# A hybrid decoder layer on one core: x's tiles loaded in another sequence, and the table of priority shifts replaced for all three stages

## Chip, core and metric

The kernel runs on one core of a Trainium2 chip. A core has TensorE (matrix products, PE in the profile), VectorE (DVE), ScalarE (ACT), GpSimd (POOL), SyncE (SP, which issues most transfers), and 16 DMA engines between the chip's main memory and the core's memories, SBUF for operands and PSUM for the results of TensorE. The metric is the time of one execution on the device in microseconds, here the median of three runs.

## The reference, cut to what matters

All data is float32. x is 1024 x 1024, and 16 meta tokens stand ahead of it, so 1040 rows go through one layer:

```python
h = rms_norm(x, pre_norm_g)
z = h @ W_in                                        # 1024 x 7328
pv, pg, cq, ckv, kr, mg, cu, cg, sbcx, sg, gl = split_cols(z)
y_a = (pool_mixer(pv) * silu(pg)) @ w_out_pool      # windows 2, 4, 8, 16, mean minus self
y_b = (mla_attention(cq, ckv, kr) * silu(mg)) @ w_out_mla    # 8 heads, causal softmax
y_c = (conformer_conv(cu) * silu(cg)) @ w_out_conf  # width 31, LayerNorm, swish
y_d = (short_conv(sbcx) * silu(sg)) @ w_out_sc      # width 3
g = sigmoid(gl + gate_bias)                         # four gates for each channel
out = x + rms_norm((g0*y_a + g1*y_b + g2*y_c + g3*y_d) @ W_o, post_norm_g)
```

## The kernel before

**Products.** A float32 operand is split into a high part (rounded to the format that TensorE multiplies fast, `fp32r` in the profile) and a low part, the rest. `split` lets ACT copy the high part and another engine, POOL where nothing is said, subtract for the low part. A product then takes three matmuls: high by high, high by low, low by high. The two large products, with W_in and W_o, use a scheme of Strassen's kind: seven products of blocks instead of eight, whose operands are blocks or sums of blocks.

**Stage 1** (up to the first `plan.flush()`, L1579) loads x in eight tiles of 128 rows (`load_x`, L903) and the meta tokens. `parts` (L957) handles one or more tiles: `square` (L934) forms the sum of squares on ACT (`junk` in the profile), POOL forms the reciprocal root, `scaled` lets DVE scale the tile (`x<-x,rsx,ps`), and `operand_of` (L946) transposes it on TensorE (`ps_x` and `ps_y` from `ident,x`), with the high part copied by ACT and the low part subtracted by DVE. Tiles 0 to 3 go into the operands B11 and B21, tiles 4 to 7 into B12 (whose memory is also called T3) and B22. `sums_of` (L969) forms the sums for T1, T2 and T4 on POOL and DVE. Then come

- `plain` (L779): the columns of `ckv` and `kr`, with eight products in the banks `ps_pa` and `ps_pb` for each of two column ranges, U0 and U1 (256 columns, and 256 with the 16 of the meta tokens). Within a range it goes through (B11, B21), tiles 0 to 3, and then (B12, B22), tiles 4 to 7.
- 28 pairs of weight blocks. `prep` (L693) splits the weights of a pair (`A` and `S` in the profile, sums `ss` and `raw` on DVE, low parts on POOL), and `unit` (L734) runs the seven products into `ps_pa`, `ps_pb`, `ps_pc` and `ps_pd`; DVE and ACT take the results (`u`, `z`). The last pair's results, gates, go to memory tiles `zlast`, which POOL stores.
- side work between the units: the convolutions, the query and key columns, the pool tasks (`task_pool`, L1232: POOL adds shifted rows `sa` and `sb`, DVE subtracts, `ps_y<-sa,pv` and `ps_y<-sb,pv`), and others.

**Stage 2** (up to L1878) is attention over 8 heads and two halves of the queries (`attend`, L1684): scores into five banks `ps_s`, ACT's exponential `p`, its split `pt`, products with `vt` into the one bank `ps_o`, which ACT copies out (`ol`). Key blocks of 128 end in one of 16 rows (`100x16`). Between them TensorE does the output products of the three other branches (`ps_y<-bo,whl`). Stage 2's memory overlies stage 1's: `ol` lies where `zlast` was. **Stage 3** is the product with W_o, the second norm and the output.

**What sets the order.** No line issues an instruction at once. `Plan.record` (L352) notes each operation with its number, an estimated cost and what it depends on; the whole program is recorded so, and issued through one line, L389, which is why all rows of the profile name it. `flush` (L549) orders the operations of a stage by a simulation of the five engines: whenever an engine is free, it takes, among the operations that are ready by the modelled times, the one with the lowest priority number. That is the operation's number, less a lift that `plan.ahead(n)` gives. The table SHIFTS then adds to the numbers of single operations or runs of them: an entry is (first operation in the stage, how many, engine or None for all, by how much). Before, it has 55 entries for stage 2 and 7 for stage 3, none for stage 1. Where TensorE has nothing ready and the first pair's units are not over yet, the simulation puts filler transposes into its order, up to eight in a row (`keep_busy`, L307; `ps_w<-ident`).

On the chip every engine runs its list in the order that came out of this, and waits where an operand, a bank or a slot of memory isn't there yet.

Of the kernel before, what the change touches and what calls it, by code (L numbers as in the profile page):

```python
# [23 lines left out]
BF16 = mybir.dt.bfloat16  # L24
AF = mybir.ActivationFunctionType
ALU = mybir.AluOpType
# [4 lines left out]
P = 128  # L31
D = 1024
# [21 lines left out]
C_CU, C_CG, C_SC, C_SG, C_GL = 1440, 1952, 2208, 2976, 3232  # L54
# [8 lines left out]
B11, B21, B22, T1, T2, T3, T4 = range(7)  # L63

B12 = T3
# [6 lines left out]
def f(ap):  # L72
    return ap.bitcast(F32)

SHIFTS = {
    2: [
        (515, 16, "PE", -400), (164, 16, "PE", 60), (1048, 32, None, -5), (1358, 64, "DVE", 5),  # L80
        (1663, 8, None, 150), (1490, 64, "POOL", -5), (1072, 32, "DVE", -5), (1524, 16, "POOL", -150),
        (1874, 2, None, 60), (144, 2, "PE", 20), (886, 16, "DVE", 5), (660, 16, "PE", 20), (1595, 32, "PE", -60),
        (1866, 2, "PE", 150), (1322, 16, "DVE", -5), (1186, 8, "PE", -60), (1425, 8, None, -150),
        (1014, 32, "DVE", -400), (1874, 4, "ACT", -60), (15, 4, "SP", -20), (1916, 4, None, -60),
        (1936, 4, None, -20), (1299, 64, "PE", -5), (1492, 16, None, 20), (1323, 4, "DVE", 20), (1492, 1, None, 5),
        (1642, 32, "PE", -5), (1090, 2, "DVE", 20), (1907, 32, "POOL", 400), (901, 1, "DVE", 400),
        (1762, 16, "PE", -400), (1849, 32, None, -60), (1784, 16, "PE", 60), (182, 8, "PE", -400),
        (1903, 8, "PE", 150), (1582, 4, "PE", 20), (1237, 1, None, -20), (252, 2, "DVE", 400),
        (1491, 16, "PE", -150), (890, 64, "POOL", -20), (133, 8, "PE", -150), (980, 4, None, 5),
        (1938, 2, None, 150), (1291, 4, "PE", -150), (1496, 64, "PE", 5), (968, 16, None, -20),  # L90
        (1206, 32, "POOL", -400), (653, 64, "PE", -5), (1617, 32, "PE", 20), (1764, 32, "DVE", 60),
        (1691, 8, "PE", -400), (1596, 64, "PE", -20), (1847, 16, "PE", 20), (1332, 2, None, -400),
        (1218, 16, "PE", 20),
    ],
    3: [
        (433, 16, "PE", -20), (139, 16, "POOL", 400), (860, 32, "DVE", -150), (814, 32, "PE", 60),
        (600, 8, "PE", 60), (809, 16, "DVE", 400), (762, 2, None, -20),
    ],
}

# [139 lines left out]
class Plan:  # L240
# [308 lines left out]
    def flush(self):  # L549
# [9 lines left out]
        self.phase += 1  # L559
        for a, n, eng, by in SHIFTS.get(self.phase, ()):  # L560
            for o in ops[a:a + n]:
# [10 lines left out]
def trunk_kernel(ctx, tc, a):  # L572
    nc = tc.nc
    plan = Plan(nc)
    PE, ACT, DVE, POOL, SP = (plan.engine(e) for e in ("PE", "ACT", "DVE", "POOL", "SP"))
# [10 lines left out]
    def copy(out, in_, scale=1.0):  # L586
        ACT.activation(out, in_, AF.Copy, scale=scale)

    def sub(eng, out, x, y):
        eng.tensor_tensor(out, x, y, op=ALU.subtract)  # L590
# [7 lines left out]
    def split(hi, lo, src, eng=None):  # L598
        copy(hi, src)
        sub(eng or POOL, lo, src, f(hi))  # L600
# [65 lines left out]
    tp = pool(one, name="tp", reuse_waits="tile")  # L666
# [18 lines left out]

        return wp.tile([P, KH, 2 * P], F32, tag="raw", bufs=3, name=name)

    def blk(src, name):
        b = wp.tile([P, 2, KH, P], F32R, tag="blk", bufs=7, name=name)
        split(b[:, 0], b[:, 1], src)  # L690
        return b

    def prep(c):  # L693

        (a11, a21), (a12, a22) = ((t[:, :, :P], t[:, :, P:]) for t in (wload(0, c), wload(1, c)))
        ss = raw("ss")
        s1, s2 = ss[:, :, :P], ss[:, :, P:]  # L700
        add(DVE, s1, a21, a22)
        sub(DVE, s2, s1, a11)
        sub(DVE, a21, a11, a21)
        w = {n: blk(src, n) for n, src in (("A11", a11), ("S2", s2), ("S1", s1), ("S3", a21))}
        sub(DVE, s2, a12, s2)
        w.update({n: blk(src, n) for n, src in (("A12", a12), ("A22", a22), ("S4", s2))})
        return w

    def product(ps, w, b, c0, n, start, stop):
# [66 lines left out]
            out(0, 1, pc, u2[:, :nb], u2)  # L776
        pump()

    def plain(w, c0, n, out):  # L779

        for j, bs in enumerate(((B11, B21), (B12, B22))):
            for i, m in enumerate((P, 64)):
                ps = bank(("pa", "pb")[i])[:m, :n if j == 0 else min(n, 512 - c0)]
                for h, b in enumerate(bs):
                    (product, stacked)[i](ps, w[h][i], b, c0, n, h == 0, h == 1)
                with plan.ahead(EVAC):
                    out(i, j, ps, None, None)
# [113 lines left out]
    xt = {}  # L901

    def load_x(t):  # L903

        xt[t] = (t4([P, D], name="x") if t in (4, 5, 6, 7) else
                 wp.tile([P, D], F32, tag="raw", bufs=3, name="x") if t == 0 else
                 wp.tile([P, D], F32, tag="blk", bufs=7, name="x"))
        for c in (slice(0, 512), slice(512, D)) if t == 0 else (slice(0, D),):
            SP.dma_start(xt[t][:, c], a["x"][0, P * t:P * (t + 1), c])
    g8 = tp.tile([KD, P], F32, tag="wraw", bufs=2, name="g8")  # L910

    with plan.slow(-2000):
        load_x(0)
        ACT.dma_start(g8, a["pre_norm_g"][0].rearrange("(k p) -> k p", p=P))
        load_x(1)
        load_x(4)
        load_x(5)
        raw_kv = [wload(i, C_CKV, P + 32) for i in range(2)]
        for t in (2, 6, 3, 7):
            load_x(t)  # L920
        xm = wp.tile([NM, D], F32, tag="blk", bufs=7, name="xm")
        SP.dma_start(xm, a["meta_tokens"])
# [8 lines left out]
    ssx = const.tile([P, 16], F32, name="ssx")  # L931
    rsx = const.tile([P, 16], F32, name="rsx")

    def square(x_, t):  # L934
        n = x_.shape[0]
        ACT.activation(tp.tile([P, D], BF16, tag="whl", name="junk")[:n], x_, AF.Square, accum_out=ssx[:n, t:t + 1])

    def scaled(x_, t):
        n = x_.shape[0]
# [14 lines left out]
        copy(HB[b][:, 0, :, c], p3)  # L954
        sub(DVE, HB[b][:, 1, :, c], p3, f(HB[b][:, 0, :, c]))

    def parts(*ts):  # L957

        r0 = turn[1]
        turn[1] += len(ts)  # L960
        for i, t in enumerate(ts):
            square(xt[t], r0 + i)
        rsqrt_mean(rsx[:, r0:r0 + len(ts)], ssx[:, r0:r0 + len(ts)], D, eng=POOL)
        for i, t in enumerate(ts):
            scaled(xt[t], r0 + i)
            for j, b in enumerate(((B11, B21), (B12, B22))[t // 4]):
                operand_of(b, t % 4, xt[t][:, 512 * j:512 * (j + 1)])
# [36 lines left out]
    U0, U1 = (0, 256), (256, 256 + NM)  # L1004

    def nopump():
        pass
    parts(0)
    parts(1)

    w_kv = [[blk(t[:, :, :P], "kv")] for t in raw_kv]
    kr = wp.tile([P, 2, KH, 64], F32R, tag="blk", bufs=7, name="kr")
    for i, t in enumerate(raw_kv):
        split(kr[:, i, :, :32], kr[:, i, :, 32:], t[:, :, P:P + 32])
        w_kv[i].append(kr[:, i])
    parts(4, 5)
    out_kv = [out_raw(("ckv", "kr"), *u) for u in (U0, U1)]
    parts(2, 6)
    parts(3, 7)
    meta()  # L1020
    plain(w_kv, *U0, out_kv[0])
    for t in range(2):
        sums_of(t)
    w = prep((C_CU, C_CU + 256))
    for t in range(2):
        operand_of(T3, t, xt[t + 4][:, :512])
    for t in range(2, 4):
        sums_of(t)
    plain(w_kv, *U1, out_kv[1])
    for t in range(2, 4):  # L1030
        operand_of(T3, t, xt[t + 4][:, :512])
    prow = w1([P, P], name="prow")
# [530 lines left out]
    for i, (_, names, kind) in enumerate(pairs):  # L1563
# [11 lines left out]
        w = nxt  # L1575
# [381 lines left out]
    for d in (0, 4, 1, 5, 2, 6, 3, 7):  # L1957
        whl = [wtile(ep, "w_out_mla", d, i) for i in range(2)]
        th = ep.tile([P, NT], F32, tag="th", bufs=3, name="th")
        ld(th, th_dram[8 + d])  # L1960
        for c in range(2):
            t = th[:, 512 * c:512 * (c + 1)]
            py = bank("u")
            for k in range(4):
                b = boM[c][k]
                w = whl[k // 2][:, :, k % 2]
# [154 lines left out]
```

## Time and profile before

| what | us |
|---|---|
| median of three runs | 962.89 (961.86 to 963.99) |
| the profiled execution | 961.49 |
| its span in the trace | 959.6 |
| TensorE busy | 943.1 |
| VectorE, ScalarE, GpSimd busy | 700.4, 451.8, 675.7 |
| DMA | 205.95 MB, 215 GB/s on average |

A row of a timeline reads: start and length in us, engine, line, operation, result<-operands, shape, how many in a row, and in brackets how long the engine had been idle and what released it. A group's row ends in busy us and mean ns of one, then the idle time ahead of it. `L389` is the recording line throughout.

### The profile page before, as it was taken

What the parts mean: (1) busy time and instruction counts of PE and PEld (TensorE: products, weight loads), DVE (VectorE), ACT (ScalarE), POOL (GpSimd) and SP (SyncE); (2) the same over time, 40 slices, a digit from 0 to 9 for tenths busy, and PEclk for the clock granted to TensorE, in tenths of its full rate; (3) what the DMA queues carried; (4) which work ended last, traced back from release to release, by engine and by line L of the source; (5) the groups of instructions that cost most, each with busy time, mean ns of one, the idle gap of its engine ahead of it and who ended that gap; (6) DMA issues with size and microseconds to landing.
All of it is one profiled execution on the core that took longest, in us unless ns stands there. A gap on an engine that the chain in (4) does not pass through costs nothing.

```text
span 959.6 us, 15213 instructions
## 1 busy us (share of the span) xinstructions
PE 943.1 (98%) x4944; PEld 803.2 (84%) x4944; DVE 700.4 (73%) x1124; ACT 451.8 (47%) x925; POOL 675.7 (70%) x627
## 2 busy tenths in 40 slices
PE   8999999999999999999999999989999999999996
PEld 7998999988888888888888888868888888888885
DVE  5855988896998898555665558437868887898656
ACT  7753344334443454554554443256465564325622
POOL 5957677557877776778876886456368796847955
PEclk9999999999999999999999999999999999999998
DMA  8146556666688959868696578798978864783533
GB/s 262 42 127 204 148 185 216 219 216 230 227 254 266 315 189 279 243 186 240 213 281 186 148 238 294 221 293 241 292 210 270 209 209 127 259 282 113 178 124 146
DMA packets 143875, 205.95 MB, mean 215 GB/s; under 512 B 21169, under 2 KB 88752, under 8 KB 143028
## 3 DMA queue, kind: packets, MB, share of 16 engines
q1 hardware_dynamic: 134820, 188.20, 63.4%
q10 hardware_dynamic: 8656, 15.74, 4.5%
q0 software_dynamic: 320, 1.05, 0.3%
q8 instruction: 39, 0.64, 0.3%
q14 instruction: 40, 0.33, 0.1%
HBM read 132.01 MB, written 72.89 MB: 214 GB/s over the span
## 4 chain that ended last, share of the span: by engine, by line
PE 91%; DMA 2%; DVE 2%; issue 1%; POOL 1%; ACT 1%; SPq 0%; DVEq 0%; ACTq 0%; POOLq 0%
PE ps_pa L389 16%; PE ps_pb L389 15%; PE ps_pc L389 14%; PE ps_o L389 10%; PE ps_y L389 8%; PE ps_u L389 8%; PE ps_pd L389 7%; PE ps_s L389 7%; PE ps_x L389 4%; DVE ps_w L389 1%; DMA kt<-k 1%; DMA x<-in_x_dram 1%; SPq L389 0%; POOL S L389 0%; DMA th<-z 0%
## 5 line engine op out<-in xcount | busy, mean ns | idle before, releaser
L389 PE MATMUL ps_pb<-T,S 128*128 128x512 f32 (+2 forms) x792 | 171.0, 358 | 1.0 <-DVE u L389 1.0
L389 PE MATMUL ps_pa<-B,A 128*128 128x512 f32 (+2 forms) x792 | 169.2, 358 | 0.0
L389 POOL TENSOR_TENSOR S<-ss,S 128x512 fp32r<-128x512 f32 x84 | 114.8, 1378 | 57.9 <-ACT S L389 55.7
L389 PEld LDWEIGHTS ps_pb<-T,S 128*128 128x128 f32 x792 | 133.8, 189 | 22.8 <-DVE u L389 1.2
L389 PEld LDWEIGHTS ps_pa<-B,A 128*128 128x128 f32 x792 | 134.0, 188 | 21.6 <-DVE z L389 0.4
L389 POOL TENSOR_TENSOR pt<-p,pt 128x512 fp32r<-128x512 f32 (+2 forms) x96 | 104.3, 1112 | 46.7 <-PE ps_s L389 24.6
L389 POOL TENSOR_TENSOR A<-raw,A 128x512 fp32r<-128x512 f32 x84 | 112.8, 1355 | 34.0 <-ACT A L389 34.0
L389 DVE TENSOR_TENSOR u<-ps_pb,u 128x512 f32<-128x512 f32 (+2 forms) x66 | 40.4, 612 | 76.4 <-PE ps_pb L389 61.1
L389 DVE SCALAR_TENSOR_TENSOR ps_w<-conv,par,ps_w 128x512 f32<-128x512 f32 x116 | 87.2, 752 | 2.5
L389 PE MATMUL ps_y<-bo,whl 128*128 128x512 f32 x288 | 86.3, 405 | 0.0
L389 PE MATMUL ps_pc<-T,S 128*128 128x512 f32 (+1 forms) x396 | 84.9, 357 | 0.0
L389 PE MATMUL ps_pd<-T,A 128*128 128x512 f32 (+2 forms) x396 | 84.5, 358 | 0.0
L389 PE MATMUL ps_pc<-B,S 128*128 128x512 f32 (+1 forms) x396 | 83.0, 357 | 0.0
L389 PEld LDWEIGHTS ps_pc<-B,S 128*128 128x128 f32 x396 | 67.3, 188 | 11.0 <-issue 0.2
L389 PEld LDWEIGHTS ps_pd<-T,A 128*128 128x128 f32 x396 | 67.3, 188 | 11.0 <-issue 0.2
L389 PEld LDWEIGHTS ps_pc<-T,S 128*128 128x128 f32 x396 | 67.0, 189 | 10.9
L389 ACT ACTIVATE p<-ps_s 128x512 f32<-128x512 f32 (+4 forms) x112 | 49.2, 443 | 53.4 <-PE ps_s L389 32.7
L389 PE MATMUL ps_o<-pt,vt 128*128 128x512 f32 (+7 forms) x288 | 67.9, 345 | 2.5 <-ACT ol L389 2.1
L389 PE MATMUL ps_s<-qt,kt 100*128 100x512 f32 (+7 forms) x336 | 68.6, 323 | 0.6 <-ACT p L389 0.6
L389 ACT ACTIVATE S<-ss 128x512 fp32r<-128x512 f32 x84 | 50.5, 627 | 33.2 <-DVE ss L389 18.9
L389 ACT ACTIVATE z<-z,par 128x512 f32<-128x512 f32 x45 | 32.5, 721 | 66.2 <-DVE z L389 65.3
L389 PEld LDWEIGHTS ps_s<-qt,kt 100*128 100x128 f32 (+2 forms) x336 | 54.4, 176 | 10.8 <-ACT p L389 0.9
(298 smaller groups left out, 1908.0 us busy)
## 6 DMA issues: line engine op xcount, KB each, us to landing
raw<-in_w_in_dram SPq DMA_DIRECT2D x52, 512.0 KB
th<-th SPq DMA_DIRECT2D x32, 512.0 KB
th<-z ACTq DMA_DIRECT2D x60, 256.0 KB
v<-vhl SPq DMA_DIRECT2D x16, 384.0 KB
qt<-q SPq DMA_DIRECT2D x16, 384.0 KB
vt<-v SPq DMA_DIRECT2D x8, 768.0 KB
bo<-bo SPq DMA_DIRECT2D x6, 1024.0 KB
w_out_mla<-whl SPq DMA_DIRECT2D x16, 256.0 KB
```

Source lines behind the costliest of these rows:

```text
L389: getattr(self.handle[o["eng"]], o["op"])(*map(real, o["args"]), **{k: real(v) for k, v in o["kw"].items()})
```

## The change

1. x's tiles and the first weights are loaded in the sequence x0, x1, the two kv weight blocks, x4, x5, x6, x7, x2, x3, meta; it was x0, x1, x4, x5, kv weights, x2, x6, x3, x7, meta. The tiles are worked on as (0), (1), (4), (5), (6, 7), (2, 3); it was (0), (1), (4, 5), (2, 6), (3, 7).
2. Tile 4's sum of squares is one DVE operation (128x1024) instead of an ACT one.
3. `plain` goes through tiles 4 to 7 first for U1. Its products are the same.
4. In the first pair's `prep`, three of seven low parts (S2, S3, A22) are subtracted on DVE instead of POOL.
5. SHIFTS has 66 entries for stage 1, 239 for stage 2 (other ones than before) and 29 for stage 3.

TensorE's instructions are the same but for the fillers, 63 before and 50 after; of these, 24 and 12 stand behind the first product.

```diff
 SHIFTS = {
+    1: [
+        (98, 1, "PE", -803), (111, 1, "PE", -2854), (150, 1, "PE", -328), (223, 1, "PE", -1373),
...
     2: [
-        (515, 16, "PE", -400), (164, 16, "PE", 60), (1048, 32, None, -5), (1358, 64, "DVE", 5),
...
+        (29, 3, "PE", -3289), (38, 1, "PE", -3289), (43, 2, "PE", 2919), (51, 1, "PE", 2304), (67, 2, "PE", 965),
...
-    def blk(src, name):
+    def blk(src, name, eng=None):
         b = wp.tile([P, 2, KH, P], F32R, tag="blk", bufs=7, name=name)
-        split(b[:, 0], b[:, 1], src)
+        split(b[:, 0], b[:, 1], src, eng)
         return b
 
-    def prep(c):
+    def prep(c, engs=(None, None)):
...
-        w = {n: blk(src, n) for n, src in (("A11", a11), ("S2", s2), ("S1", s1), ("S3", a21))}
+        w = {n: blk(src, n, engs[i % 2]) for i, (n, src) in enumerate((("A11", a11), ("S2", s2), ("S1", s1), ("S3", a21)))}
         sub(DVE, s2, a12, s2)
-        w.update({n: blk(src, n) for n, src in (("A12", a12), ("A22", a22), ("S4", s2))})
+        w.update({n: blk(src, n, engs[i % 2]) for i, (n, src) in enumerate((("A12", a12), ("A22", a22), ("S4", s2)))})
...
-    def plain(w, c0, n, out):
+    def plain(w, c0, n, out, order=(0, 1)):
 
-        for j, bs in enumerate(((B11, B21), (B12, B22))):
+        for j in order:
+            bs = ((B11, B21), (B12, B22))[j]
...
         load_x(1)
-        load_x(4)
-        load_x(5)
         raw_kv = [wload(i, C_CKV, P + 32) for i in range(2)]
-        for t in (2, 6, 3, 7):
+        for t in (4, 5, 6, 7, 2, 3):
             load_x(t)
...
-    def square(x_, t):
+    def square(x_, t, eng=ACT):
         n = x_.shape[0]
-        ACT.activation(tp.tile([P, D], BF16, tag="whl", name="junk")[:n], x_, AF.Square, accum_out=ssx[:n, t:t + 1])
+        junk, s = tp.tile([P, D], BF16, tag="whl", name="junk")[:n], ssx[:n, t:t + 1]
+        if eng is DVE:
+            DVE.scalar_tensor_tensor(junk, x_, 1.0, x_, op0=ALU.mult, op1=ALU.mult, accum_out=s)
+        else:
+            ACT.activation(junk, x_, AF.Square, accum_out=s)
...
-    parts(4, 5)
+    parts(4, eng=DVE)
+    parts(5)
     out_kv = [out_raw(("ckv", "kr"), *u) for u in (U0, U1)]
-    parts(2, 6)
-    parts(3, 7)
+    parts(6, 7)
+    parts(2, 3)
     meta()
     plain(w_kv, *U0, out_kv[0])
     for t in range(2):
         sums_of(t)
-    w = prep((C_CU, C_CU + 256))
+    w = prep((C_CU, C_CU + 256), (POOL, DVE))
...
-    plain(w_kv, *U1, out_kv[1])
+    plain(w_kv, *U1, out_kv[1], (1, 0))
```

What this does to the order is shown at three places.

**TensorE in the start.** Transposes of x's tiles (`ps_x`, `ps_y`), fillers (`ps_w`) and plain products (`ps_pa` for ckv, `ps_pb` for kr) before, where the last of the first eight products is over and the meta tokens (`xm`) come:

```order
L389 MATMUL ps_pb<-B_332,kr 32x256
L389 MATMUL ps_w<-ident 128x128 x3
L389 MATMUL ps_x<-ident,x 128x128 x4
L389 MATMUL ps_w<-ident 128x128 x5
L389 MATMUL ps_y<-ident,x 128x128 x4
L389 MATMUL ps_w<-ident 128x128 x2
L389 MATMUL ps_x<-ident,x 128x128 x4
L389 MATMUL ps_w<-ident 128x128 x6
L389 MATMUL ps_x<-ident,xm 128x16 x4
```

And after, up to the same transposes of the meta tokens (T_361 is T3, the operand of tiles 4 to 7, and B_368 is B22):

```order
L456 MATMUL ps_x<-ident,x 128x128 x4
L456 MATMUL ps_pa<-T_361,kv 128x256 x6
L456 MATMUL ps_pa<-B_368,kv 128x256 x2
L456 MATMUL ps_x<-ident,x 128x128 x4
L456 MATMUL ps_pa<-B_368,kv 128x256 x3
L456 MATMUL ps_y<-ident,x 128x128 x3
L456 MATMUL ps_pa<-B_368,kv 128x256 x5
L456 MATMUL ps_y<-ident,x 128x128
L456 MATMUL ps_pb<-T_361,kr 64x256
L456 MATMUL ps_pb<-T_361,kr 32x256
L456 MATMUL ps_x<-ident,xm 128x16 x4
```

Products of tiles 4 to 7 stand between the transposes where fillers stood. Ahead of this, at the first product, 13 fillers around two products became 18 around two.

**DVE at the first pool task.** The two pool operations (`ps_y`), the sums of the next pair's weights (`ss`), and the operation that frees a product's bank (`u2` from `ps_pb`) before:

```order
L389 SCALAR_TENSOR_TENSOR ps_y_1854<-sa_1827,pv_1652 64x512
L389 SCALAR_TENSOR_TENSOR z_1845<-z_1825,z_1845 128x256
L389 TENSOR_TENSOR z_1845<-ps_pc_1767,u2_1794 128x256
L389 SCALAR_TENSOR_TENSOR z_1845<-z_1825,z_1845 128x256
L389 TENSOR_TENSOR ss_1899<-raw_1731,raw_1773 128x4x128
L389 TENSOR_TENSOR ss_1899<-ss_1899,raw_1731 128x4x128
L389 TENSOR_TENSOR u2_1919<-ps_pb_1835,u3_1889 128x272
```

And after:

```order
L456 SCALAR_TENSOR_TENSOR z_1825<-z_1813,z_1825 128x256
L456 TENSOR_TENSOR z_1825<-ps_pc_1734,u2_1778 128x256
L456 SCALAR_TENSOR_TENSOR z_1825<-z_1813,z_1825 128x256
L456 SCALAR_TENSOR_TENSOR ps_y_1875<-sa_1823,pv_1618 64x512
L456 SCALAR_TENSOR_TENSOR ps_y_1875<-sb_1845,pv_1618 64x512
L456 TENSOR_TENSOR u2_1899<-ps_pb_1818,u3_1871 128x272
L456 TENSOR_TENSOR ss_1906<-raw_1723,raw_1772 128x4x128
L456 TENSOR_TENSOR ss_1906<-ss_1906,raw_1723 128x4x128
```

The sums went behind the `u2`, and both pool operations stand ahead of it.

**TensorE from stage 1 to stage 2.** The last unit's products and the first scores before:

```order
L389 MATMUL ps_pd<-T_595,A_6717 128x512 x12
L389 MATMUL ps_pa<-B_262,A_6711 128x512 x12
L389 MATMUL ps_pc<-B_332,S_6722 128x512 x12
L389 MATMUL ps_s<-qt,kt_6927 128x512 x3
L389 MATMUL ps_s<-qt,kt_6927 128x272 x2
```

And after:

```order
L456 MATMUL ps_pd<-T_626,A_6703 128x512 x12
L456 MATMUL ps_pa<-B_248,A_6697 128x512 x3
L456 MATMUL ps_pc<-B_368,S_6709 128x512 x12
L456 MATMUL ps_pa<-B_248,A_6697 128x512 x9
L456 MATMUL ps_s<-qt,kt_6917 128x512 x3
```

The product in `ps_pc` went ahead of nine of the twelve matmuls in `ps_pa`, so a result in `ps_pa`, not in `ps_pc`, is the last of stage 1. Behind this, up to the first `ps_o` of the second unit, 15072 score columns stand where 11408 stood.

## Prediction before the run

> **What bounds the kernel now.** I read the page first, then the waits of TensorE, then busy time by stretches, then the timelines at the places that these name. The page's head and its chain:
>
> ```profile
> span 959.6 us, 15213 instructions
> PE 943.1 (98%) x4944; PEld 803.2 (84%) x4944; DVE 700.4 (73%) x1124; ACT 451.8 (47%) x925; POOL 675.7 (70%) x627
> ...
> PE 91%; DMA 2%; DVE 2%; issue 1%; POOL 1%; ACT 1%; SPq 0%; DVEq 0%; ACTq 0%; POOLq 0%
> ```
>
> TensorE is busy 98% of the span and is 91% of the chain. Its products are the same before and after, so only three things can give time: TensorE's idle time, filler transposes that count as busy, and pairs of matmuls that run slower than their own pitch. The longest waits of TensorE (engine, tile, releaser: us in total, times, longest) and three stretches of the start (busy us and count of PE, PEld, DVE, ACT, POOL, then granted clock, DMA share, GB/s) say where:
>
> ```profile
> PE ps_o L389 <- ACT ol L389: 2.1, 1, 2.1
> PE ps_w L389 <- POOL ident masks.py:199: 1.4, 1, 1.4
> PE ps_pb L389 <- DVE u L389: 1.0, 1, 1.0
> ```
>
> ```profile
> 20.00:30.00 10.00, 10.00 (x90) 9.94 (x89) 9.49 (x15) 8.18 (x19) 9.43 (x11) 1.00 0.24 72
> 30.00:40.00 10.00, 9.37 (x79) 8.67 (x78) 9.08 (x17) 6.32 (x15) 9.61 (x9) 1.00 0.06 13
> 40.00:50.00 10.00, 10.00 (x88) 9.69 (x87) 7.58 (x10) 7.93 (x16) 9.92 (x9) 1.00 0.28 86
> ```
>
> The second wait, of a filler for its constant, lies ahead of all products and is not touched. Four places are left: the start up to 34 us, one wait of 1.0 us at 147 us, the passage from stage 1 to stage 2 with the 2.1, and pairs of small and large matmuls in stage 2. Elsewhere TensorE is full, and a new order can only lose.
>
> **The start** (load order, tile 4's square sum, plain products, phase 1's shifts). TensorE's timeline:
>
> ```profile
> 13.27 0.51 PE L389 MATMUL ps_pa<-B,kv 128*128 128x256 f32 x2 [0.76 <-ACT kv L389]
> 13.61 0.71 PE L389 MATMUL ps_w<-ident 128*128 128x128 f32 x5
> 14.40 0.63 PE L389 MATMUL ps_y<-ident,x 128*128 128x128 f32 x4
> ...
> 27.95 0.49 PE L389 MATMUL ps_w<-ident 128*128 128x128 f32 x3
> 28.28 0.60 PE L389 MATMUL ps_x<-ident,x 128*128 128x128 f32 x4
> ...
> 33.14 0.33 PE L389 MATMUL ps_w<-ident 128*128 128x128 f32 x1
> ```
>
> The first product waits for the split of the kv weights on ACT, then five fillers (`ps_w`) run; the unbroken stream begins at 14.40. From 27.95 to 33.14 there are 19 more fillers, first and last shown. The first three take 28.28 − 27.95 = 0.33 us, 0.11 each, so the 19 are 2.1 us of nothing; 10 − 9.37 = 0.6 us of idle time lies among them.
>
> The change loads the kv weights ahead of x4 and x5 and takes x4's square from in front of their split on ACT. In the new order one `kv` product, one `kr` product and 11 fillers stand ahead of the stream, and what they wait for is tile 1's low half from DVE, not ACT. I put the stream at 13.4, 1.0 us sooner (at best 14.40 − 13.27 = 1.1). Later, the 19 fillers are replaced by products of tiles 4 to 7, one filler is left: at best 2.1 + 0.6 = 2.7. At best 3.8 together.
>
> DVE, the supplier of every low half, pays for it. Its prices stand in its own timeline around 140 us, which is needed again below, and in the row of the operation nearest to the square:
>
> ```profile
> 139.07 2.88 DVE L389 SCALAR_TENSOR_TENSOR ps_y<-sa,pv 64x512 f32<-64x512 f32 x1 [0.31 <-POOL sa L389]
> 141.88 1.27 DVE L389 SCALAR_TENSOR_TENSOR z<-z 128x256 f32<-128x256 f32 x1
> 143.08 0.41 DVE L389 TENSOR_TENSOR z<-ps_pc,u 128x256 f32<-128x256 f32 x1
> 143.52 0.42 DVE L389 SCALAR_TENSOR_TENSOR z<-z 128x256 f32<-128x256 f32 x1
> 143.86 0.68 DVE L389 TENSOR_TENSOR ss<-raw 128x512 f32<-128x512 f32 x1
> 144.58 1.67 DVE L389 TENSOR_TENSOR ss<-ss,raw 128x512 f32<-128x512 f32 x1
> 146.17 0.43 DVE L389 TENSOR_TENSOR u<-ps_pb,u 128x272 f32<-128x272 f32 x1
> ```
>
> ```profile
> L389 DVE SCALAR_TENSOR_TENSOR ckv<-ckv,par,rsb 128x1040 f32<-128x1040 f32 x1 | 1.3, 1291 | 0.0
> ```
>
> One form has two prices there: `z<-z` 0.42 and 1.27, a 128x512 `ss` 0.68 and 1.67, the longer ones beside work on POOL. DVE gets tile 4's square sum, which the trace of before doesn't show on it: 1.29 by the nearest row (`ckv`, 1040 wide), three times that (3.9) at the longer price. It also gets three of the first pair's seven low-half subtractions (128x512): 2.0 us at 0.68, 5.0 at 1.67. From 20 to 50 us DVE idles 0.51 + 0.92 + 2.42 = 3.85. The middle price of the subtractions, 3.5, just fits, and POOL, 94 to 99% busy there, is freed of three of its own. The square comes when tile 4 lands, ahead of 13 us and next to tile 1's low half; I take its short price, since its place is in the start's own wait. Of the 3.8 I take 2.7 as kept and about 1 as come back in waits for DVE. **Start: −2.7, at best −3.8.** At worst nothing is gained, the subtractions overrun by 5.0 − 3.85 = 1.2 and the square delays the stream by 3.9 − 1.3 = 2.6: +3.8.
>
> The Trainium skill ("SBUF — State Buffer", section "Who interferes with whom") speaks against this part: a DVE instruction with two SBUF inputs and a GpSimd instruction that reads SBUF take a shared port in turn, and the later one waits for all of the other's time. The two prices of one form agree with it. By that rule all three subtractions would take the long price, and the start would give about 1.5 us less than I take.
>
> **The wait at 147 us** (phase 1's shifts). In the timeline above DVE frees the bank `ps_pb` (its `u` at 146.17) only after 7.1 us of other work that began at 139.07, and TensorE lost 1.0. The new order puts the two `ss` operations (0.68 + 1.67 = 2.35) behind the `u`, and the pool task's second operation, `ps_y<-sb`, ahead of it. The eight operations of this kind in the kernel:
>
> ```profile
> L389 DVE SCALAR_TENSOR_TENSOR ps_y<-sa,pv 64x512 f32<-64x512 f32 x4 | 6.8, 1698 | 2.1 <-POOL sa L389 2.0
> L389 DVE SCALAR_TENSOR_TENSOR ps_y<-sb,pv 64x512 f32<-64x512 f32 x4 | 4.4, 1106 | 0.1
> ```
>
> At these means the queue is 7.1 − 2.35 − 2.88 + 1.70 + 1.11 = 4.7 us and the wait is gone: −1.0. With 2.88 for each and both `z<-z` at 1.27 it is 7.1 − 2.35 + 2.88 + 0.85 = 8.5: +1.4. I take **−0.6**. The same pair stands ahead of a `u` a second time, at the third pool task, where TensorE did not wait: 0, at worst the whole +2.4 (8.5 less the 6.1 that TensorE bore above without waiting).
>
> **The passage to stage 2** (phases 1 and 2). Stage 1 ends on TensorE at 627.77 + 2.88 = 630.65; call it E. TensorE, ACT, POOL, and the landing of the four `zlast` stores:
>
> ```profile
> 627.77 2.88 PE L389 MATMUL ps_pc<-B,S 128*128 128x512 f32 x12
> ...
> 638.18 0.87 PE L389 MATMUL ps_s<-qt,kt 100*128 100x512 f32 x3
> 641.17 0.50 PE L389 MATMUL ps_o<-pt,vt 128*128 128x512 f32 x1 [2.12 <-ACT ol L389]
> ```
>
> ```profile
> 631.42 0.72 ACT L389 ACTIVATE zlast<-zlast,par 128x512 f32<-128x512 f32 x1 [2.70 <-DVE zlast L389]
> ...
> 640.52 0.60 ACT L389 ACTIVATE ol<-ps_o 128x512 f32<-128x512 f32 x1 [2.83 <-DMA th<-zlast]
> ```
>
> ```profile
> 632.43 0.54 POOL L389 DMA_DIRECT2D th<-zlast  x1 [2.88 <-ACT zlast L389]
> ```
>
> ```profile
> DMA to landing us min/median/max: 5.5/7.3/8.0
> ```
>
> ACT's copy `ol` overwrites the memory of the last `zlast`, so it waits until that store has landed: issued at E + 1.8, landed 8.0 later. TensorE ran out of score products at 639.05 and stood 2.12 us. In the new order the last product is `ps_pa`, nine of its matmuls behind `ps_pc`, and its `zlast` is one ACT operation instead of a DVE and an ACT one, so the store is issued about 0.7 sooner (E + 1.1) and lands between E + 6.6 and E + 9.1. ACT has two `p` and one `pt` more ahead of `ol` (some 1.8 us at 0.6 each, the price of a 128x512 copy), which fill its wait of 2.83: `ol` starts near E + 9.0 instead of E + 9.87. Between E and the second unit's first `ps_o` TensorE has 15072 score columns instead of 11408 (added up from the two orders); 3664 more, at 2.88 / 12 = 0.24 us for 512, are 1.7 us of work moved ahead. So TensorE comes 1.7 later and finds `ol` 0.9 sooner: the 2.12 go but for about 0.1. **−2.0 (−0.5 to −3.0)**: the low end with TensorE's banks held by ACT's `p`, the high end if smaller waits beside it, which I put at 1 us, go too.
>
> **Pairs in stage 2** (phase 2's shifts). TensorE in one unit:
>
> ```profile
> 749.91 0.23 PE L389 MATMUL ps_s<-qt,kt 100*16 100x16 f32 x3
> 749.99 0.48 PE L389 MATMUL ps_y<-bo,whl 128*128 128x512 f32 x1
> ```
>
> The matmul behind three 16-wide ones ends 750.47 − 750.14 = 0.33 us after them, against the pitch of 0.24: 0.09 lost. Eight heads times two halves make 16 such triples, at most 1.4 us. In the new order about half of them stand ahead of matmuls that load 64 columns and not 128: **−0.7 (0 to −1.4)**.
>
> **Elsewhere.** Phase 3's shifts reorder the last parts, and the output behind the last matmul stays as long: 0. The 334 table entries move products in full stretches, where a misplaced one costs a wait like the 1.0 at 147 us; I expect half of one: **+0.5 (0 to +1.5)**.
>
> **The sum.** −2.7 − 0.6 − 2.0 − 0.7 + 0.5 = −5.5. The profiled execution took 961.49 (span 959.6 and 1.9 around it), 1.4 below the median of the runs, 962.89. It comes to 956.0 profiled, and to **957.4** as a median.
>
> **The rivals.**
> 1. *DVE's supply takes the start's gain back.* For it: DVE is 91 to 95% busy from 20 to 40 us and gets up to 5.0 more. Against: POOL is relieved. The 2.7 are lost: −2.8, 960.1. Chance 0.17.
> 2. *The passage still waits*: for a store of 8 us, or for banks that ACT frees late. The 2.0 stay: 959.4. For it: stores that took 5.5 to 8.0. Against: 1.7 more of work ahead of the wait. Chance 0.13.
> 3. *Slower: POOL holds up DVE wherever the change puts a DVE operation with two SBUF inputs beside it.* Start +3.8, 147 us +1.4, third pool task +2.4 are 7.6; passage and pairs still give 2.7: +4.9, 967.8. It decides from 2.7 us of hold-ups on. For it: the doubled and trebled rows. Against: it needs most of these operations at their worst row, while `ps_y` has means of 1.7 and 1.1. Chance 0.08.
> 4. *The order changes little on the chip*: the gains of start and passage both go, −0.8: 962.1. It was made with modelled times, and holds only where they do. Chance 0.12.
> 5. *The clock.* The granted clock is 1.00 in all three stretches above, fillers or not. If a hole long enough to lower it came with rival 1, and, say, 3.4 us behind it ran at half speed, 1.7 us would come on top: 961.8. Beside it, the Trainium skill ("TensorE: Matmul & The Clock Gate", "Part 1: The HAM clock gate") says that an idle window of about 3.4 us halves the clock until TensorE has been busy as long again; the longest hole in these rows, 2.12 us, is shorter, and the order leaves none that I expect longer. Chance 0.02.
>
> **How the numbers follow.** My own case has 0.48. A measurement of this kernel can tell about 0.2% (1.9 us) from no change, so faster is below 961.0 and slower above 964.8. Faster: 0.48, of rival 1 0.13, of rival 2 0.12, of rival 4 0.02, together 0.75. Slower: rival 3 and 0.01 of the rest, 0.09. The same: 0.16. Range: all terms at their good ends are −3.8 − 1.0 − 3.0 − 1.4 = −9.2, 953.7, put at 953.5; the upper end takes in rivals 1, 2, 4 and 5: 962.5. That leaves out rival 3 and what is unforeseen.
>
> **What would show it.** Start: one `ps_w` left between 20 and 34 us, and the first `ps_pa<-B,A` some 3 us earlier; waits of TensorE on DVE's `T` or `B` or on `S` of over 1 us there are rival 1. At 147 us: no wait of `ps_pb` on DVE's `u`. Passage: `ps_o` waits for `ol` under 0.5 us. `ps_y` rows near 2.9 with waits of `ps_pb` of several us are rival 3. I am wrong if TensorE's waits grow in stretches that were full, or if the time is outside 953.5 to 962.5.

## Result, and the profile after

The changed kernel takes 955.65 us (median of 4 runs, 954.15 to 957.07), before 963.44 (4 runs, 961.86 to 964.7): 7.8 us less, ratio 0.9923 with a 95% interval of 0.9905 to 0.9940. Forecast were 957.4 and 953.5 to 962.5. The two profiled executions differ by less: 961.49 and 956.06, spans 959.6 and 954.3. One profiled execution further down, of the kernel without the 19 fillers, fell into a slower state and took 2418 us, so no trace of that kernel is used. Head and chain of the page after:

```profile
span 954.3 us, 15157 instructions
...
PE 940.4 (99%) x4931; PEld 803.4 (84%) x4931; DVE 697.0 (73%) x1129; ACT 450.4 (47%) x923; POOL 672.6 (70%) x626
...
PE 95%; DMA 2%; DVE 2%; POOL 1%; issue 0%; ACT 0%; SPq 0%; DVEq 0%; POOLq 0%; ACTq 0%
```

The waits of TensorE (us in total, times, longest):

```profile
PE ps_x L456 <- DVE x L456: 1.5, 1, 1.5
PE ps_w L456 <- POOL ident masks.py:199: 1.4, 1, 1.4
PE ps_pb L456 <- DVE u L456: 0.6, 1, 0.6
PE ps_s L456 <- DVE mxs L456: 0.6, 1, 0.6
PE ps_pa L456 <- ACT u L456: 0.3, 1, 0.3
```

The 2.1 us of `ps_o` for `ol` are gone, and so is the 1.0 of `ps_pb` for `u` at 147 us; the 0.6 in the third row is another one, at 175 us. To see where the span's 5.3 us come from, I add up for each stretch what TensorE lost: for every matmul the time from the end of the one ahead to its own end, less the least that its shape takes in these traces (5th percentile), with fillers counted whole. The two sums differ by 5.25, as do the ends of the last matmul (951.23 and 945.98).

| stretch | lost before | after | difference | forecast |
|---|---|---|---|---|
| start, 0 to 60 us | 14.26 | 11.99 | -2.3 | -2.7 |
| wait at 147 us (130 to 160) | 1.95 | 0.70 | -1.25 | -0.6 |
| rest of stage 1 | 5.62 | 7.78 | +2.2 | part of +0.5 |
| passage, 625 to 660 us | 6.13 | 2.30 | -3.8 | -2.0 |
| stage 2 from 660 us on | 9.13 | 9.11 | 0 | -0.7, part of +0.5 |
| stage 3 | 0.41 | 0.37 | 0 | 0 |

**Start.** TensorE's timeline up to the unbroken stream:

```profile
12.02 0.66 PE L456 MATMUL ps_x<-ident,x 128*128 128x128 f32 x4
12.51 0.93 PE L456 MATMUL ps_w<-ident 128*128 128x128 f32 x7
13.20 0.37 PE L456 MATMUL ps_pa<-B,kv 128*128 128x256 f32 x1
13.40 1.04 PE L456 MATMUL ps_w<-ident 128*128 128x128 f32 x8
14.20 0.36 PE L456 MATMUL ps_pb<-B,kr 128*64 128x256 f32 x1
14.40 0.49 PE L456 MATMUL ps_w<-ident 128*128 128x128 f32 x3
14.64 1.55 PE L456 MATMUL ps_pa<-B,kv 128*128 128x256 f32 x11
```

Seven rows without one wait in brackets: fillers run back to back, and the stream starts at 14.64, not at 13.4. The gain lies behind it: of the 19 fillers one is left (at 21.52), and from 26 to 36 us TensorE lost 3.7 us before and 1.1 after.

**147 us.** DVE's queue at the same place:

```profile
139.33 0.69 DVE L456 SCALAR_TENSOR_TENSOR ps_y<-sa,pv 64x512 f32<-64x512 f32 x1
140.12 0.70 DVE L456 SCALAR_TENSOR_TENSOR ps_y<-sb,pv 64x512 f32<-64x512 f32 x1
140.85 0.44 DVE L456 TENSOR_TENSOR u<-ps_pb,u 128x272 f32<-128x272 f32 x1
141.21 1.30 DVE L456 TENSOR_TENSOR ss<-raw 128x512 f32<-128x512 f32 x1
```

Both pool operations take 0.7 each, and the `u` that had come at 146.17 comes at 140.85. A new wait stands at the second pool task. DVE, then TensorE:

```profile
171.88 0.81 DVE L456 TENSOR_SCALAR ps_w<-conv,par 128x512 f32<-128x512 f32 x1
172.60 2.29 DVE L456 SCALAR_TENSOR_TENSOR ckv<-ckv,par,rsb 128x1040 f32<-128x1040 f32 x1
174.82 0.41 DVE L456 TENSOR_TENSOR u<-ps_pb,u 128x256 f32<-128x256 f32 x1
```

```profile
175.29 0.98 PE L456 MATMUL ps_pb<-T,S 128*128 128x256 f32 x6 [0.62 <-DVE u L456]
```

`ckv` took 1.29 us before and takes 2.29 here, ahead of the `u` that TensorE needs.

**Passage.** TensorE, ACT, POOL, and the landing of the four `zlast` stores (us, least, median, most):

```profile
627.07 2.20 PE L456 MATMUL ps_pa<-B,A 128*128 128x512 f32 x9
629.11 3.00 PE L456 MATMUL ps_s<-qt,kt 100*128 100x512 f32 x18
...
638.99 1.77 PE L456 MATMUL ps_o<-pt,vt 128*128 128x512 f32 x7
```

```profile
629.31 0.69 ACT L456 ACTIVATE zlast<-ps_pa,par 128x512 f32<-128x512 f32 x1 [0.53 <-PE ps_pa L456]
...
637.91 0.60 ACT L456 ACTIVATE ol<-ps_o 128x512 f32<-128x512 f32 x1
```

```profile
630.29 0.54 POOL L456 DMA_DIRECT2D th<-zlast  x1 [0.68 <-ACT zlast L456]
```

```profile
DMA to landing us min/median/max: 7.0/7.7/8.3
```

Stage 1 ends at 629.27, so 1.4 us of the 5.25 come from stage 1 as a whole, and 3.9 from behind it. `ol` starts 8.6 us after that end without any wait of ACT (9.9 before), and TensorE comes to the second unit's `ps_o` when it is done. The store is no faster than before. It was close: by the trace the last store landed at 637.81, 0.1 us ahead of `ol`. One that took 9.0 us, as the slowest of the runs below did, would have held ACT up by some 1.4 us (an estimate: 630.29 + 9.0 − 637.91).

### The profile page after: what moved, and what is told of

It reads as the page before. It is cut to its first block, busy times and chain, and to the rows that moved or that the text cites. A ratio compares the mean times of both kernels' runs of the same rounds, so it can differ in the third digit from the quotient of the medians.

```text
span 954.3 us, 15157 instructions
## 1 busy us (share of the span) xinstructions
PE 940.4 (99%) x4931; PEld 803.4 (84%) x4931; DVE 697.0 (73%) x1129; ACT 450.4 (47%) x923; POOL 672.6 (70%) x626
## 4 chain that ended last, share of the span: by engine, by line
PE 95%; DMA 2%; DVE 2%; POOL 1%; issue 0%; ACT 0%; SPq 0%; DVEq 0%; POOLq 0%; ACTq 0%
PE ps_pa L456 17%; PE ps_pb L456 17%; PE ps_pc L456 16%; PE ps_o L456 10%; PE ps_pd L456 8%; PE ps_u L456 8%; PE ps_s L456 8%; PE ps_y L456 7%; PE ps_x L456 4%; DMA x<-in_x_dram 1%; DMA raw<-in_w_in_dram 1%; DMA whl<-w_out_mla 1%; DVE ps_y L456 0%; PE ps_w L456 0%; DVE ckv L456 0%
## 5 line engine op out<-in xcount | busy, mean ns | idle before, releaser
L456 PE MATMUL ps_pa<-B,A 128*128 128x512 f32 (+2 forms) x792 | 172.3, 358 | 0.3 <-ACT u L456 0.3
L456 POOL TENSOR_TENSOR pt<-p,pt 128x512 fp32r<-128x512 f32 (+3 forms) x96 | 101.9, 1084 | 50.0 <-ACT pt L456 19.6
L456 PE MATMUL ps_y<-bo,whl 128*128 128x512 f32 x288 | 82.9, 398 | 0.0
L456 PE MATMUL ps_s<-qt,kt 100*128 100x512 f32 (+8 forms) x336 | 68.9, 325 | 0.3 <-ACT p L456 0.3
L456 PEld LDWEIGHTS ps_s<-qt,kt 100*128 100x128 f32 (+3 forms) x336 | 53.2, 176 | 10.6 <-ACT p L456 1.1
L456 PEld LDWEIGHTS ps_y<-bo,whl 128*128 128x128 f32 x288 | 52.1, 189 | 8.3 <-issue 0.2
```

The source lines that it names most:

```text
L456: getattr(self.handle[o["eng"]], o["op"])(*map(real, o["args"]), **{k: real(v) for k, v in o["kw"].items()})
```

## The experiments

In these kernels each engine's list of operations is taken from one of the two kernels' plans and replayed as it stands, so that an entry can be moved and nothing else moves with it. The core of that edit, the same in all:

```diff
-        r = self.simulate(prio, ops)
+        lists = {e: unpacked(t) for e, t in ORDERS[self.phase].items()} if self.phase in ORDERS else None
+        r = self.simulate(prio, ops, lists)
```

With lists, the simulation gives an engine the next operation of its list, or a filler, when that can start. Below, only what differs from the kernel named is shown. Ratios are to before, run beside them (medians 962.67, 963.19 and 963.17 in the three groups).

### Which stage's order wins the passage

The changed kernel's order of stage 2 on before's stage 1:

```diff
 # before.py
+ORDERS = {2: the changed kernel's lists, 3: before's lists}
```

> Stage 1 in the order of before, stage 2 in the changed kernel's order, stage 3 as before. Theory A (the passage is won by stage 2's order: 1.7 us of score products and ACT work moved ahead of the first copy of ps_o): the wait of ps_o on ol falls from 2.1 to under 0.8 us, and the time is 2 to 3 us below before; stage 2 behind 660 us is worth nothing. Rival B (it is won by stage 1's end, which issues the last store sooner): the wait stays above 1.3 us and the gain is about 1 us.

Measured: 961.27 us, ratio 0.9990 (0.9977 to 1.0003). No row of TensorE waits for `ol` any more: the mechanism is A's. At the passage, from 625 to 660 us, TensorE loses 4.0 us, 2.1 less than before and 1.7 more than the changed kernel. It waits 1.6 us for `qt<-q` instead; SP's loads come later than in the changed kernel (`kt<-kr` issued at 621.64, not 614.38). The time doesn't show these 2.1, and the trace says where they go: behind 831 us TensorE loses 4.4 us in this execution, against 0.4 both before and in the changed kernel. There before's list of stage 3 follows a stage 2 that it wasn't made for. TensorE there, and three stretches of 3.41 us (the second value of a row is TensorE's busy time, the third from the end the granted clock):

```profile
831.66 0.97 PE L470 MATMUL ps_u<-boM,whl 128*128 128x512 f32 x3 [0.98 <-ACT boM L470]
833.46 8.89 PE L470 MATMUL ps_u<-boM,whl 128*128 128x512 f32 x31 [0.83 <-POOL boM L470]
```

```profile
830.01:833.42 3.41, 1.64 (x6) 0.67 (x4) 0.50 (x1) 1.26 (x2) 3.41 (x4) 1.00 0.98 345
833.42:836.83 3.41, 3.37 (x8) 2.69 (x9) 2.08 (x3) 1.56 (x3) 2.53 (x3) 0.50 1.04 412
836.83:840.25 3.42, 3.42 (x16) 2.81 (x16) 1.90 (x4) 0.96 (x2) 1.29 (x1) 1.00 0.41 125
```

Two waits of 1.8 us together left TensorE busy for 1.64 us of the first stretch, and through the next one the clock was 0.50: 3.41 x 0.5 = 1.7 us more.

The complement, the changed kernel's stage 1 with the other two stages in before's order:

```diff
 # after.py
+ORDERS = {2: before's lists, 3: before's lists}
```

> The changed kernel's stage 1, stages 2 and 3 in the order of before. Theory A: start -2.3, wait at 147 us -1.3, new waits in stage 1 +2.3, passage about -0.8: 2 us below before, with ps_o still waiting over 1 us for ol. Rival B: the passage gives 3 of its 3.8 here, 4.3 us below before, with that wait gone.

Measured: 959.67 us, ratio 0.9967 (0.9957 to 0.9977), 3 us below before, between the two theories' times. The wait decides, and it is A's:

```profile
639.86 0.50 PE L536 MATMUL ps_o<-pt,vt 128*128 128x512 f32 x1 [2.13 <-ACT ol L536]
```

TensorE loses 6.2 us from 625 to 660, as before, so this stage 1 alone gives nothing at the passage. There the gain is 2.1 us with stage 2's order alone, 0 with stage 1's alone, and 3.8 with both. The ratios of the two kernels, 0.9990 x 0.9967 = 0.9957 against 0.9923 for the whole change, don't show how much the stages need each other: neither has the changed stage 3, and the first pays 4 us at a border that the changed kernel doesn't have.

### The last product and the last store

In before, and reversed in the changed kernel, the last two products of stage 1 are swapped, with the two gates on ACT and their stores on POOL:

```diff
 # before.py, TensorE's list of stage 1, end
-ps_pa<-B,A 128x512 x12
+ps_pa<-B,A 128x512 x3
 ps_pc<-B,S 128x512 x12
+ps_pa<-B,A 128x512 x9
```

> Before, with the last product of stage 1 (ps_pc) put ahead of nine matmuls of the one before it (ps_pa), and ACT's and POOL's last two gates swapped to match; all else in the order of before. Theory A: the last store is issued 0.7 us sooner, ol starts 0.7 to 0.9 sooner, the wait of 2.1 falls to 1.2 to 1.4: 0.8 us below before. Rival B: the wait goes entirely, 2 us or more.

Measured: 961.58 us, ratio 0.9991 (0.9981 to 1.0002). ACT's `ol`, and TensorE:

```profile
638.23 0.60 ACT L539 ACTIVATE ol<-ps_o 128x512 f32<-128x512 f32 x1 [0.28 <-PE ps_o L539]
```

```profile
645.96 0.47 PE L539 MATMUL ps_y<-bo,whl 128*128 128x512 f32 x1 [0.89 <-DMA whl<-w_out_pool]
...
647.93 0.54 PE L539 MATMUL ps_s<-kt,qt 96*128 96x328 f32 x2 [0.61 <-DMA qt<-q]
```

The last store landed early enough this time (3.9 to 7.2 us), the wait for `ol` went entirely, as B had it, and the time did not: loads of weights and queries are late next. TensorE's loss from 625 to 660 is 5.9, hardly below the 6.1 of before.

```diff
 # after.py, TensorE's list of stage 1, end
-ps_pa<-B,A 128x512 x3
+ps_pa<-B,A 128x512 x12
 ps_pc<-B,S 128x512 x12
-ps_pa<-B,A 128x512 x9
```

> The changed kernel with the last two products of stage 1 back in the order of before (ps_pa whole, then ps_pc), and ACT's and POOL's last two gates swapped to match. If the passage is won by stage 2's order and its loads (theory A), the last store comes 0.7 us later and ol waits at most 0.5 us: within 0.2% of the changed kernel. If the earlier store is what counts (rival B), the wait of ps_o on ol is back with 1.5 to 2 us and the time 2 us above.

Measured: 955.19 us, ratio 0.9918 (0.9903 to 0.9932), no difference from the changed kernel. A store took up to 9.0 us, and `ol` again started at ACT's own pace:

```profile
637.48 0.58 ACT L611 ACTIVATE ol<-ps_o 128x512 f32<-128x512 f32 x1
```

So the earlier store, a step of my working, has no gain that these runs can tell. What counts is that ACT and TensorE have other work for the time that the store takes, and that the loads for that work are there.

```diff
 # before.py
-            POOL.dma_start(half(th_dram[g + i], j), z)
+            ACT.dma_start(half(th_dram[g + i], j), z)
```

> Before, with the four stores of zlast issued by ACT instead of POOL, right behind the operation that makes each; all else in the order of before. If the wait is a matter of POOL's way of issuing (theory P), such a store lands in under 5 us, ol starts at once when ACT comes to it, and the 2.1 us go: 2 us below before. If the DMA engines are full there (their share is 0.99 and more from 630 to 650 us; theory D), the store lands about as late, 6 us or more, and the wait stays above 1 us.

Measured: 976.93 us, ratio 1.0150 (1.0136 to 1.0164): neither. The queue's own waits:

```profile
SPq L538 <- DMA th<-zlast: 15.0, 4, 8.9
```

Issued by ACT, these stores stand in the way of SP's loads for stage 2, which wait 15.0 us for them; in before, SP has no wait for these stores. The kernel's own model counts the transfers of SP and ACT together, at most eight in flight, and leaves out POOL's (L444 of before), and in the trace the landings of SP's and ACT's transfers are told by the same eight semaphores in turn, those of POOL's by others. So a load waits for the store that stands eight places ahead of it, even while ACT hasn't issued that store yet. ACT's first store, and the load that waited 8.9 us for it (issued at 611.17 in before):

```profile
624.99 0.33 ACTq L538 DMA_DIRECT2D th<-zlast  x1
```

```profile
627.01 0.56 SPq L538 DMA_DIRECT2D kt<-k  x1
```

TensorE then waits 5.8 and 5.5 us for `qt` and `kt`, and the clock is 0.50 for 17.07 us (635.22 to 652.29). The two rows also bound that store's landing: 2.0 us after its issue, where POOL's in before took 5.5 to 8.0. But the DMA engines' share was 0.35 from 625 to 627 us, not near 1.0 as there. Issuer and load differ at once, so P and D stay open.

### Fillers, loads and DVE's share at the start

```diff
 # before.py, TensorE's list: the last 19 fillers
-ps_w<-ident 128x128 x3
...
-ps_w<-ident 128x128 x1
```

> Before, without the 19 fillers between 27.95 and 33.14 us; nothing else moves. Theory A (the fillers stand in waits for transposes' banks and DVE, so they are a sign of lost time and not its cause): TensorE waits there instead, the first unit starts as before, no change within 0.2%. Rival B (they hold up what comes behind them): up to 2.1 us below before. If the clock needs them, the granted clock falls under 1.00 from 30 to 40 us and the time rises.

Measured: 964.15 us, ratio 1.0005 (0.9994 to 1.0017). By these times, A: the fillers mark time that is lost in any case. What gains is the products in their place.

```diff
 # after.py
-    w = prep((C_CU, C_CU + 256), (POOL, DVE))
+    w = prep((C_CU, C_CU + 256))
```

> The changed kernel with the three low parts of the first pair back on POOL, in POOL's order right behind the low part ahead of each; all else in the changed kernel's order. Theory A (DVE had room, and POOL is what the first unit waits for): TensorE waits 1 to 3 us for S or A between 45 and 55 us. Rival B (DVE pays for them): DVE is freed of 2.9 us (0.68, 1.56 and 0.68 in the changed kernel) and the time falls by up to 1 us.

Measured: 961.53 us, ratio 0.9983 (0.9973 to 0.9992), 6 us above the changed kernel. TensorE, POOL, and two stretches of 3.41 us:

```profile
50.09 1.10 PE L611 MATMUL ps_pc<-T,S 128*128 128x256 f32 x7 [3.44 <-POOL S L611]
```

```profile
43.38 1.29 POOL L611 TENSOR_TENSOR S<-ss,S 128x512 fp32r<-128x512 f32 x1 [5.57 <-ACT S L611]
```

```profile
44.96:48.37 3.41, 1.69 (x15) 1.41 (x12) 2.32 (x3) 2.40 (x6) 3.33 (x4) 1.00 0.00 0
48.37:51.79 3.42, 1.70 (x15) 1.71 (x15) 0.05 (x1) 0.00 (x0) 3.42 (x5) 1.00 0.34 115
```

B is out: freeing DVE gained nothing. The wait accounts for half of the 6 us: this profiled execution, the fastest of the twelve, took 958.86 us, 2.8 above the changed kernel's, at a mean clock of 0.998, and in both stretches that the wait lies in the clock was 1.00. The eleven others took 960.54 to 962.59 at 0.993 to 0.996. A lowered clock behind the wait could explain them (see the last section), but their traces weren't kept. Besides, the size is partly of my making: I put the first of the three where POOL had to stand 5.57 us for ACT's high part, with sums for other operands behind it. A better place on POOL was not tried, so how much the move to DVE is worth stays open.

```diff
 # after.py, SP's list of stage 1, beginning
 x<-in_x_dram x3
+x<-in_x_dram x1
 raw<-in_w_in_dram x2
-x<-in_x_dram x6
+x<-in_x_dram x5
```

> The changed kernel with x4 loaded ahead of the two kv weight blocks; all else in its order. If the kv weights' load delays x1 (theory K), x1's square starts near 6.5 instead of 7.86 and the stream of products near 13.6 instead of 14.64: up to 1 us below the changed kernel. If x1's landing merely differs from run to run, as it does between runs of one order (6.51, 7.48 and 7.89 in three kernels with the load order of before; theory V), nothing changes beyond 0.2%.

Measured: 957.06 us, ratio 0.9943 (0.9930 to 0.9955). x1's square began at 5.89, the earliest of all, and the stream at 14.56 all the same: now the kv weights come late, and TensorE waits 0.6 us for POOL's `kr` and 1.1 for `B`. One landing doesn't decide between K and V, and the time doesn't either: its interval overlaps the changed kernel's.

```diff
 # after.py
-    parts(4, eng=DVE)
+    parts(4)
```

> The changed kernel with tile 4's square sum on ACT, ahead of tile 5's; all else in its order. Theory A (the square on DVE, 1.42 us, stands in front of tile 1's last low part and the stream waits for that): the stream starts 0.5 us sooner, tile 4's operands come up to 0.5 later, the time stays within 0.2%. Rival B (ACT is the scarcer engine at the start): products of tile 4 wait, 0.5 to 1 us above the changed kernel.

Measured: 954.35 us, ratio 0.9911 (0.9898 to 0.9924): the changed kernel's time within the intervals, so DVE's square is not needed. Its 1.42 us (1.29 estimated) did no harm either. x1's square began at 6.88 and the stream at 13.66: 6.78 later, exactly as in the changed kernel (7.86 and 14.64).

```diff
 # the kernel of the run above, TensorE's list: the last 12 fillers
 ps_pa<-B,kv 128x256 x1
-ps_w<-ident 128x128 x8
 ps_pb<-B,kr 64x256 x1
-ps_w<-ident 128x128 x3
 ps_pa<-B,kv 128x256 x11
...
-ps_w<-ident 128x128 x1
```

> The changed kernel with tile 4's square on ACT as in the run before it, and without the 12 fillers behind the first product. In four kernels of the changed order the stream of products starts 6.78 us after x1's square begins, with the square of tile 4 on DVE or on ACT: theory F says that the 11 fillers ahead of it, run without a gap, hold it there, so without them it starts 6.2 us after x1 (when DVE's low part is there), 0.5 us sooner. Rival G: it is set by x1's own chain (square, root, scaling, transposes, low part), 6.7 to 6.8 us as before, and nothing changes within 0.2%. If the clock needs the fillers, it shows under 1.00 from 10 to 20 us.

Measured: 954.86 us, ratio 0.9914 (0.9899 to 0.9929), no change. TensorE:

```profile
13.19 1.58 PE L611 MATMUL ps_pa<-B,kv 128*128 128x256 f32 x12
15.81 0.63 PE L611 MATMUL ps_y<-ident,x 128*128 128x128 f32 x4 [1.04 <-issue]
```

F was right about the fillers and wrong about the gain. The stream starts 5.67 us after x1's square (7.52), 1.1 sooner, and then TensorE stands 1.04 us for tile 4's transposes, which come 8.29 us after x1's square, as they did with the fillers (15.17 − 6.88 = 8.29). DVE, just ahead of them:

```profile
14.97 0.75 DVE L611 SCALAR_TENSOR_TENSOR x<-x,rsx,ps_pc 128x512 f32<-128x512 f32 x1 [1.26 <-POOL rsx L611]
```

DVE waits for POOL's root of tile 4 and then scales the tile, up to 15.72. So here the start is set by tile 4's own chain of square, root and scaling.

### The new waits

```diff
 # after.py, DVE's list at 172 and at 203 us
-ps_w<-conv,par
 ckv<-ckv,par,rsb
 u<-ps_pb,u
+ps_w<-conv,par
...
-ps_w<-conv,par,ps_w x2
 pdl<-ps_y,pdh
+ps_w<-conv,par,ps_w x2
```

> The changed kernel with three of the convolution's operations moved back in DVE's list: one behind the u that TensorE waits for at 175 us, two behind the pdl that it waits for at 206 us. If these new waits (0.6 and 0.2 us, 1.4 of lost time with what lies around them) are misplaced operations on DVE, both go: 0.8 to 1.3 us below the changed kernel. If DVE is merely full there, other operations become late and nothing is won.

Measured: 955.32 us, ratio 0.9919 (0.9905 to 0.9934). The wait at 175 us is gone (lost from 160 to 190: 1.13 instead of 1.74), the 0.2 at 206 us is still there, and a new 0.5 of `ps_x` for DVE's `khl` stands beside it (190 to 220: 1.17 instead of 0.92): 0.4 us won by the trace, nothing that the times can tell. DVE is full there (busy for 28.2 of 30 us from 160 on and 29.0 of 30 from 190 on, in the changed kernel); a moved operation makes another late.

And the last three edits together:

```diff
 # after.py
-    parts(4, eng=DVE)
+    parts(4)
 # TensorE's list, last 12 fillers
-ps_w<-ident 128x128 x12
 # DVE's list at 172 and at 203 us
-ps_w<-conv,par
 ckv<-ckv,par,rsb
 u<-ps_pb,u
+ps_w<-conv,par
...
-ps_w<-conv,par,ps_w x2
 pdl<-ps_y,pdh
+ps_w<-conv,par,ps_w x2
```

> All edits of actsq_nf and waits together. If they add up: 1.5 to 2 us below the changed kernel, near 953.7. If the start's 0.5 us is lost in waits for DVE later on, only the 0.8 to 1.3 of the second part remain.

Measured: 954.10 us (952.27 to 955.16), ratio 0.9900 (0.9884 to 0.9917). It is the lowest median, 1.5 us below the changed kernel's, but the intervals overlap, so it is not shown to be faster.

## Why the prediction was right

- **What bounds it.** TensorE, at four places: borne out. By the lost time the four gave 8.1 us (2.3, 1.25, 3.8, and 0.8 at the pairs), and five new waits took 3.3 back: 4.8 of the span's 5.3.
- **Start.** −2.7 forecast, −2.3 lost time less. The replacement of the 19 fillers did it. The 1.0 us from an earlier stream did not show in this pair of executions: I had put it at 13.4, it was 14.64, because x1 landed late (square at 7.86 instead of 6.53). With the changed load order the stream starts 6.78 us after x1's square, within 0.01, in the six traces that keep its loads and fillers (13.66 to 14.64 for 6.88 to 7.86); for a square at 6.53 that makes 13.3, an estimate, so the step held and the landing hid it. With before's order it starts at 14.40 to 15.01 for squares at 6.51 to 7.89 (four traces). The sign that I named, a first `ps_pa<-B,A` some 3 us earlier, was no measure of this: it came 6.5 us earlier (42.44, before 48.92), since it now stands among the plain products. DVE's price for three subtractions was 0.68 + 1.56 + 0.68 = 2.9, taken as 3.5. The one of 1.56 (at 44.86) lay beside an operation on POOL, that at 48.86 in a time when POOL stood idle, and that at 44.06 had begun 0.33 us ahead of POOL's next one, which then took 1.48 instead of 1.29. So the trace agrees with the rule of the Trainium skill on the shared port ("SBUF — State Buffer", "Who interferes with whom"), but not with all three at the long price, which I had worked out from it.
- **147 us.** The mechanism was right, the gain full (−1.25, with the loss around the wait) and not half.
- **Passage.** Mis-sized: −3.8, forecast −2.0 and at most −3.0. Right: more score products and ACT work ahead of `ol`. Wrong: the store issued sooner (no gain, by the swap and its reverse), and that the waits on `p` and `pt` beside it would stay; of 0.62 and 0.35 one of 0.31 is left. Not in my working: of the 3.8, 1.7 come only where the changed stage 1 stands ahead of the changed stage 2, with SP's loads there in time.
- **Pairs.** −0.7 forecast; matmuls behind 16-wide ones lost 1.74 us in all before (16 cases) and 0.98 after (15), −0.8. Those that load 64 columns lost 0.00 to 0.06 each, the others 0.10 to 0.12, but for one that loads 4.
- **Elsewhere.** The step that failed: "I expect half of one" wait. There are five, with 0.89 (175 us), 0.49 (206), 0.60 (311), 0.83 (698) and 0.51 (826) lost: 3.3 us, outside my bound of 1.5. That the forecast total was met in spite of it is luck: this and the passage erred in opposite directions, by 2.8 and 1.8.
- **From the profile to the median.** The sum against the profiled execution, 956.0, was met by 956.06. I then carried the same 5.5 to the median, where 7.8 were measured; 0.55 of that is a fourth run of before, which moved its median from 962.89 to 963.44. Before's profiled execution had the early x1 and was 2.0 below its median, the changed kernel's had a late one and was 0.4 above. That explains the direction. Its size, by the lost time up to 60 us: with before's load order 0.7 more for a square of x1 at 7.89 than at 6.53, with the changed one 0.8 less at 6.94 than at 7.86. The rest, with the clock of single runs as a candidate (below), is not settled.
- **Rivals.** 1 did not come: no wait on DVE's `T` or `B` above 0.3 behind the stream's start. 2 came in the experiments as late loads, and in the changed kernel it was near (the last store landed 0.1 us ahead of `ol`). 3 did not come as I had it: `ps_y` averages 0.98 and 1.27 us, at most 1.69, and never stood ahead of a wait of `ps_pb` as a pair. But its mechanism shows at 175 us, where `ckv` took 2.29 us beside operations on POOL (172.50 to 175.49 without a gap) ahead of the `u`. 5 did not come in the changed kernel's trace; in another order, where two waits came close together, it did.

## What to carry to other kernels

Where a wait at a stage's border has several causes in a row (a store's landing, loads, the next engine's queue), taking one away moves the wait: in before, the earlier store removed the wait for `ol`, and waits for loads took its place. An order for one stage also has to fit the stages beside it: the changed stage 2 ahead of before's stage 3 lost 4 us at that border. A filler or a short hole is a mark of lost time; look for the work that can stand there, and don't expect anything from removing the filler itself. And compare one profiled execution with another only after checking the first input's landing and the mean clock in both: they moved single runs by as much as these edits.

## What the runs showed of the hardware

- **What a wait costs in clock depends on where it falls.** Two waits of 0.98 and 0.83 us within 2.8 us were followed by 3.41 us at half the clock, 1.7 us of work (830 to 837 us, rows above). The wait of 3.44 us in the run with the subtractions on POOL lowered nothing (two rows there). In all thirteen traces used here the recorded stretches of lowered clock begin a whole number of steps of 3.41 us behind the start of the clock's record, and the stretches above are such steps. The wait of 3.44 us lay half in one step and half in the next. Every fall of the clock follows a step in which TensorE was busy for 1.64 us or less, and none follows one with 1.69 or more. The Trainium skill ("TensorE: Matmul & The Clock Gate", "Part 1: The HAM clock gate") speaks of an idle window of about 3.4 us; the traces agree with the length, but a step that was idle for about half was enough.
- **Single runs follow the mean clock.** Of 29 runs of before in one group, three with a mean granted clock of 0.994 took 964.5 us on average, ten with 0.997 took 961.9. In before's profiled execution (0.997) the clock is lowered only behind the last matmul, from 954.4 us on, where it costs nothing; 0.003 less is 2.9 us of the span (an estimate: 0.003 x 960), close to the 2.6. Where in these runs the clock fell was not traced.
- **POOL's stores of 256 KB** took 3.9 to 9.0 us to land, with the DMA engines' share near 1.0 (0.97 to 1.04 in before's trace from 625 to 645 us). The Trainium skill ("DMA: Bandwidth & Descriptors", "Anatomy of one DMA — SWDGE (gpsimd) path") gives 2.0 us and 436 GB/s for one alone, an estimate of 2.6 us; no run here shows one alone.
- **x1's landing** differs from run to run: its square began between 6.51 and 7.89 us in four traces with one load order.
